# RMSNorm with SiLU: each converting tile transfer cut into eight transfers of every eighth partition

## The chip, the cores and the metric

One core of a Trainium2 chip runs the whole kernel. The metric is device time in microseconds; executions of one kernel agreed within about 1% (1.4% and 1.8% in two of the experiments). The profiled execution of each kernel has its own, slightly shorter span, which the profile's shares refer to. No TensorE work is done, and the granted clock was 1.0.

## The reference

```python
batch, seq_len, hidden = 8, 1024, 2048          # x float32, gamma float32, eps 1e-5
rms = np.sqrt(np.mean(x ** 2, axis=-1, keepdims=True) + eps)
out = gamma * x / rms
return (out * (1 / (1 + np.exp(-out)))).astype(np.float32)
```

8192 rows of 2048 float32: 67.1 MB are read, 67.1 MB written. On the chip the rows are held as bfloat16, and the transfers convert both ways; both kernels issue them from POOL.

## The kernel before

A tile is 128 rows, one per partition. There are 64 tiles, each with one load and one store.

```python
pool = ctx.enter_context(tc.tile_pool(name="pool", bufs=8))
...
for i in range(ntiles):
    ...
    xt = pool.tile([P, d], bf16)
    nc.gpsimd.dma_start(out=xt[:ts], in_=x2[s:e])          # L42: float32 -> bfloat16
    xg = pool.tile([P, d], bf16)
    nc.vector.tensor_mul(out=xg[:ts], in0=xt[:ts], in1=g[:ts])
    ...                                                     # squares on DVE, Sqrt on ACT, reciprocal on DVE
    ot = pool.tile([P, d], bf16)
    nc.scalar.activation(out=ot[:ts], in_=xg[:ts], func=...Silu, scale=rstd[:ts])
    nc.gpsimd.dma_start(out=o2[s:e], in_=ot[:ts])          # L65: bfloat16 -> float32
```

## Time and profile before

| | before |
|---|---|
| time | 338.42 us median of 2 (337.41 to 339.43) |
| span of the profiled execution | 336.1 us |
| transfers issued (all from POOL) | 129 |
| POOL busy | 69.0 us, 21% |
| ACT, DVE busy | 65%, 66% |
| DMA engines' share | 104.1% |

The "share of 16 engines" adds up the time of every packet; since a row's record overlaps the next one's by 20 to 40 ns (records of 324 and 341 ns follow each other every 305 ns), it goes over 100% when the engines are always busy. GB/s counts bytes as they arrive. The prediction shows the lines.

### The profile page before, as it was taken

What the parts mean: (1) busy time and instruction counts of PE and PEld (TensorE: products, weight loads), DVE (VectorE), ACT (ScalarE), POOL (GpSimd) and SP (SyncE); (2) the same over time, 40 slices, a digit from 0 to 9 for tenths busy, and PEclk for the clock granted to TensorE, in tenths of its full rate; (3) what the DMA queues carried; (4) which work ended last, traced back from release to release, by engine and by line L of the source; (5) the groups of instructions that cost most, each with busy time, mean ns of one, the idle gap of its engine ahead of it and who ended that gap; (6) DMA issues with size and microseconds to landing.
All of it is one profiled execution on the core that took longest, in us unless ns stands there. A gap on an engine that the chain in (4) does not pass through costs nothing.

```text
span 336.1 us, 838 instructions
## 1 busy us (share of the span) xinstructions
DVE 221.2 (66%) x257; ACT 219.1 (65%) x188; POOL 69.0 (21%) x133
## 2 busy tenths in 40 slices
DVE  0999990407999914099999030899991308999900
ACT  1486977522869795238697761386978613869792
POOL 6012111050111110501111105011111050111110
DMA  7999999899999998999999989999999799999997
GB/s 140 212 214 254 335 398 363 332 312 208 214 288 327 402 365 321 324 214 214 291 316 414 366 325 310 214 212 319 307 424 367 286 297 214 213 311 309 420 429 273
DMA packets 18582, 101.24 MB, mean 301 GB/s; under 512 B 2064, under 2 KB 2064, under 8 KB 10384
## 3 DMA queue, kind: packets, MB, share of 16 engines
q0 software_dynamic: 18576, 101.20, 104.1%
q14 instruction: 6, 0.05, 0.0%
HBM read 68.16 MB, written 67.11 MB: 402 GB/s over the span
## 4 chain that ended last, share of the span: by engine, by line
issue 72%; POOL 14%; DMA 11%; POOLq 1%; PEldq 0%
DMA xt<-in_x_dram 11%; POOL out_dram L65 10%; POOL xt L42 4%; POOLq L65 0%; POOL g L34 0%; POOLq L96 0%; POOLq L42 0%; PEldq L96 0%
## 5 line engine op out<-in xcount | busy, mean ns | idle before, releaser
L48 DVE CUSTOM_DVE_ANT_0 xt<-xt 128x2048 bf16<-128x2048 bf16 x64 | 144.8, 2280 | 0.3
L45 DVE TENSOR_TENSOR xg<-xt,g 128x2048 bf16<-128x2048 bf16 x64 | 76.6, 1217 | 95.7 <-DMA xt<-in_x_dram 95.7
L62 ACT ACTIVATE ot<-xg,rstd 128x2048 bf16<-128x2048 bf16 x64 | 124.4, 1993 | 5.8 <-DVE rstd L59 5.5
L55 ACT ACTIVATE rms<-ss,eps_t 128x1 f32<-128x1 f32 x64 | 17.8, 292 | 101.8 <-DVE ss L48 63.7
L65 POOL DMA_DIRECT2D out_dram<-ot x64 | 34.2, 534 | 221.4 <-ACT ot L62 221.4
L42 POOL DMA_DIRECT2D xt<-in_x_dram x64 | 34.1, 554 | 38.8 <-DVE ss L48 22.8
L55 ACT ACT_TABLE_LOAD x30 | 38.5, 1283 | 2.1 <-DVE ss L48 1.0
L62 ACT ACT_TABLE_LOAD x30 | 38.5, 1283 | 0.5
L59 DVE RECIPROCAL rstd<-rms 128x1 f32<-128x1 f32 x64 | 8.6, 153 | 8.4 <-ACT rms L55 8.4
L48 DVE DVE_READ_ACCUMULATOR2_ANT ss<- 128x1 f32 x64 | 5.2, 81 | 0.0
L34 POOL DMA_DIRECT2D g<-in_gamma_dram x1 | 0.7, 667 | 0.8 <-PEq L96 0.8
L36 DVE MEMSET eps_t<- 128x1 f32 x1 | 0.1, 59 | 0.8 <-PEq L82 0.8
L82 POOL MEMSET const-float32-0.0<- 128x1 f32 x1 | 0.1, 99 | 0.2 <-issue 0.2
L82 POOL MEMSET const-bfloat16-1.0<- 128x1 bf16 x1 | 0.1, 102 | 0.0
L82 POOL MEMSET const-float32-1.0<- 128x1 f32 x1 | 0.1, 99 | 0.0
L82 POOL MEMSET const-uint8-127<- 128x1 uint8 x1 | 0.1, 99 | 0.0
## 6 DMA issues: line engine op xcount, KB each, us to landing
out_dram<-ot POOLq DMA_DIRECT2D x64, 1024.0 KB, 11.5
xt<-in_x_dram POOLq DMA_DIRECT2D x64, 512.0 KB, 15.5
g<-in_gamma_dram POOLq DMA_DIRECT2D x1, 512.0 KB, 4.7
```

Source lines behind the costliest of these rows:

```text
L34: nc.gpsimd.dma_start(out=g, in_=gbc)
L36: nc.vector.memset(eps_t, float(eps))
L42: nc.gpsimd.dma_start(out=xt[:ts], in_=x2[s:e])
L45: nc.vector.tensor_mul(out=xg[:ts], in0=xt[:ts], in1=g[:ts])
L48: nc.vector.tensor_tensor_reduce(out=xt[:ts], in0=xt[:ts], in1=xt[:ts], scale=1.0, scalar=0.0, op0=mybir.AluOpType.mult, op1=mybir.AluOpTy ...
L55: nc.scalar.activation(out=rms[:ts], in_=ss[:ts], func=mybir.ActivationFunctionType.Sqrt, scale=1.0 / d, bias=eps_t[:ts])
L59: nc.vector.reciprocal(out=rstd[:ts], in_=rms[:ts])
L62: nc.scalar.activation(out=ot[:ts], in_=xg[:ts], func=mybir.ActivationFunctionType.Silu, scale=rstd[:ts])
L65: nc.gpsimd.dma_start(out=o2[s:e], in_=ot[:ts])
L82: nc = _bacc.Bacc("TRN2", target_bir_lowering=False, num_devices=1)
```

## The change

The intent: a load reads 8 KB of float32 per row and writes 4 KB of bfloat16, a store the reverse. If a DMA engine can read for one while it writes for the other, then alternating single load and store rows in every engine would balance its two sides. A tile is therefore moved in eight transfers of 16 rows, which gives each of the 16 engines one row, and stores and loads are issued in turn. With it come 40 buffers, a lead of 28 loaded tiles, work in groups of four tiles, in-place tiles, and half of the squares on ACT.

```diff
+    BUFS, LEAD, GRAIN = 40, 28, 8
+    def rows(t, i, j):
+        return t[i * P:(i + 1) * P].rearrange("(p g) d -> g p d", g=GRAIN)[j]
+    def lanes(t, j):
+        ...
+        return t[j:P:GRAIN]
+    def load(i, j):
+        if j == 0:
+            xts[i] = pool.tile([P, d], bf16, name="xt")
+        nc.gpsimd.dma_start(out=lanes(xts[i], j), in_=rows(x2, i, j))
...
-        xt = pool.tile([P, d], bf16)
-        nc.gpsimd.dma_start(out=xt[:ts], in_=x2[s:e])
+    for i in range(LEAD):
+        for j in range(GRAIN):
+            load(i, j)
...
+        if k % 2 == 0:
+            nc.scalar.activation(out=sq, in_=xts[i], func=ACT.Square, accum_out=acc)
+        else:
+            nc.vector.tensor_tensor_reduce(out=junk, in0=xts[i], in1=xts[i], ...)
...
-        nc.gpsimd.dma_start(out=o2[s:e], in_=ot[:ts])
+            nc.scalar.activation(out=xt, in_=xt, func=ACT.Silu, scale=rstd[:, k:k + 1])
+            for j in range(GRAIN):
+                nc.gpsimd.dma_start(out=rows(o2, i, j), in_=lanes(xt, j))
+                if i + LEAD < ntiles:
+                    load(i + LEAD, j)
```

More of the change, by code (lines that the diff above doesn't have):

```diff
@@ L7 @@
 from concourse._compat import with_exitstack
+ACT = mybir.ActivationFunctionType
+ALU = mybir.AluOpType
 @with_exitstack
@@ L25 @@
     n, d = x2.shape
-    ntiles = (n + P - 1) // P
+    ntiles = n // P
+    BUFS, LEAD, GRAIN = 40, 28, 8
     singles = ctx.enter_context(tc.tile_pool(name="singles", bufs=1))
-    pool = ctx.enter_context(tc.tile_pool(name="pool", bufs=8))
+    pool = ctx.enter_context(tc.tile_pool(name="pool", bufs=BUFS))
     small = ctx.enter_context(tc.tile_pool(name="small", bufs=8))
+    def rows(t, i, j):
+        return t[i * P:(i + 1) * P].rearrange("(p g) d -> g p d", g=GRAIN)[j]
+    def lanes(t, j):
+        if GRAIN == 1:
+            return t
+        return t[j:P:GRAIN]
+    xts = {}
+    def load(i, j):
+        if j == 0:
+            xts[i] = pool.tile([P, d], bf16, name="xt")
+        nc.gpsimd.dma_start(out=lanes(xts[i], j), in_=rows(x2, i, j))
     g = singles.tile([P, d], bf16)
@@ L36 @@
     nc.vector.memset(eps_t, float(eps))
-    for i in range(ntiles):
-        s, e = i * P, min((i + 1) * P, n)
-        ts = e - s
-        xt = pool.tile([P, d], bf16)
-        nc.gpsimd.dma_start(out=xt[:ts], in_=x2[s:e])
-        xg = pool.tile([P, d], bf16)
-        nc.vector.tensor_mul(out=xg[:ts], in0=xt[:ts], in1=g[:ts])
-        ss = small.tile([P, 1], f32)
-        nc.vector.tensor_tensor_reduce(
-            out=xt[:ts], in0=xt[:ts], in1=xt[:ts],
-            scale=1.0, scalar=0.0,
-            op0=mybir.AluOpType.mult, op1=mybir.AluOpType.add,
-            accum_out=ss[:ts],
-        )
-        rms = small.tile([P, 1], f32)
-        nc.scalar.activation(out=rms[:ts], in_=ss[:ts],
-                             func=mybir.ActivationFunctionType.Sqrt,
-                             scale=1.0 / d, bias=eps_t[:ts])
-        rstd = small.tile([P, 1], f32)
-        nc.vector.reciprocal(out=rstd[:ts], in_=rms[:ts])
-        ot = pool.tile([P, d], bf16)
-        nc.scalar.activation(out=ot[:ts], in_=xg[:ts],
-                             func=mybir.ActivationFunctionType.Silu,
-                             scale=rstd[:ts])
-        nc.gpsimd.dma_start(out=o2[s:e], in_=ot[:ts])
+    sq = singles.tile([P, d], bf16)
@@ new lines, with stats @@
+    for i in range(LEAD):
+        for j in range(GRAIN):
+            load(i, j)
+    GROUP = 4
+    var = {}
+    def stats(i):
+        k = i % GROUP
+        if k == 0:
+            var[i // GROUP] = small.tile([P, GROUP], f32, name="ss")
+        acc = var[i // GROUP][:, k:k + 1]
+        if k % 2 == 0:
+            nc.scalar.activation(out=sq, in_=xts[i], func=ACT.Square, accum_out=acc)
+        else:
+            nc.vector.tensor_tensor_reduce(out=junk, in0=xts[i], in1=xts[i], scale=1.0, scalar=0.0,
+                                           op0=ALU.mult, op1=ALU.add, accum_out=acc)
@@ new lines, with norm @@
+    junk = singles.tile([P, d], bf16, name="junk")
+    def norm(b):
+        ss = var.pop(b)
+        rms = small.tile([P, GROUP], f32, name="rms")
+        nc.scalar.activation(out=rms, in_=ss, func=ACT.Sqrt, scale=1.0 / d, bias=eps_t)
+        rstd = small.tile([P, GROUP], f32, name="rstd")
+        nc.vector.reciprocal(out=rstd, in_=rms)
+        for i in range(b * GROUP, (b + 1) * GROUP):
+            nc.vector.tensor_mul(out=xts[i], in0=xts[i], in1=g)
+        for i in range(b * GROUP, (b + 1) * GROUP):
+            k = i % GROUP
+            xt = xts.pop(i)
+            nc.scalar.activation(out=xt, in_=xt, func=ACT.Silu, scale=rstd[:, k:k + 1])
[3 more added lines that the diff above has]
+                    load(i + LEAD, j)
@@ L69 @@
+    for b in range(ntiles // GROUP):
+        for i in range(b * GROUP, (b + 1) * GROUP):
+            stats(i)
+        norm(b)
 _INS = ['x', 'gamma', 'eps']
```

## The prediction

> **What bounds the kernel now.** I read the page's table of slices first, then the DMA queue totals, then the DMA view cut to three stretches, then the groups of instructions and the waits.
>
> The slices and the totals, over the span of 336.1 us:
>
> ```profile
> POOL 6012111050111110501111105011111050111110
> DMA  7999999899999998999999989999999799999997
> GB/s 140 212 214 254 335 398 363 332 312 208 214 288 327 402 365 321 324 214 214 291 316 414 366 325 310 214 212 319 307 424 367 286 297 214 213 311 309 420 429 273
> ...
> q0 software_dynamic: 18576, 101.20, 104.1%
> ```
>
> The DMA row is 9 nearly everywhere, so the sixteen engines are the bound. The GB/s row swings from 212 to 429 while the engines stay equally busy. The view counts bytes as they arrive: a load turns 8 KB of float32 into 4 KB, a store 4 KB into 8 KB. So 212 (all loads) and 429 (all stores) are the same rate of rows: what costs is the float32 side, whichever end it lies on.
>
> The same view in three stretches, all loads (76 to 92 us), mixed (94 to 112 us) and all stores (112 to 122 us):
>
> ```profile
> DMA packets 934, 3.40 MB, mean 212 GB/s; under 512 B 106, under 2 KB 106, under 8 KB 933
> ```
>
> ```profile
> DMA packets 1052, 5.78 MB, mean 321 GB/s; under 512 B 113, under 2 KB 113, under 8 KB 579
> ```
>
> ```profile
> DMA packets 590, 4.28 MB, mean 428 GB/s; under 512 B 66, under 2 KB 66, under 8 KB 68
> ```
>
> Packets under 512 B are the completion packets that end each transfer on each engine; the rest are rows. A row therefore holds an engine for 16 x 16.0 us / 828 = 309 ns in loads, 16 x 10.0 / 524 = 305 ns in stores, and 16 x 18.0 / 939 = 307 ns where both alternate transfer by transfer. All 16512 rows (8192 loads, 8192 stores, 128 of gamma) at 307 ns on 16 engines are 317 us; the other 19 us of the span are the start, the end, and short holes where the engines ran dry (a DMA share of 0.51 between 64 and 68 us, 0.46 between 132 and 136 us).
>
> The instructions that matter, and the waits:
>
> ```profile
> L65 POOL DMA_DIRECT2D out_dram<-ot x64 | 34.2, 534 | 221.4 <-ACT ot L62 221.4
> L42 POOL DMA_DIRECT2D xt<-in_x_dram x64 | 34.1, 554 | 38.8 <-DVE ss L48 22.8
> ```
>
> ```profile
> 1.92 3.72 POOL L42 DMA_DIRECT2D xt<-in_x_dram  x7
> ```
>
> POOL spends 0.53 us to issue one transfer of 128 rows (7 back to back in 3.72 us) and is 21% busy: 129 issues, most of its time idle behind ACT. No engine other than the DMA engines is near its limit (DVE 66%, ACT 65%).
>
> **What the Trainium skill says.** "DMA: Bandwidth & Descriptors", section "Two DMAs through the same engine are not ordered", says that an engine's read and write sides are separate queues and that descriptors are pipelined. That is the hope behind this change: a load reads 8 KB and writes 4, a store reads 4 and writes 8, so a pair needs 12 KB on each side rather than 16, and could take 3/4 of the time. The trace does not agree so far: 307 ns in the mixed stretch against 309 and 305 in the pure ones. The same page, "Anatomy of one DMA — SWDGE (gpsimd) path", says of descriptor generation that "You can emit a lot of descriptors before the incremental cost shows up"; that is, an issue costs nearly the same for few rows as for many. The trace of before has only issues of 128 rows, so it can't confirm it; it decides this case. "Perfetto Trace Analysis", section "What \"DMA-bound\" means", names the issuing engine's solid row of DMA slices as a bound of its own kind. The page on DMA, "The descriptor swizzle", has each engine of a 128-partition transfer on one SBUF port; with every eighth partition, engines n and n+4 would meet on one port. No run here shows that yet.
>
> **The change part by part.**
>
> Removed: 7/8 of the rows of each transfer. Added: 8 times as many transfers. 64 loads and 64 stores become 512 and 512, each of 16 rows, one row to an engine; with gamma 1025 issues. Rows and bytes stay.
>
> 1. Completion packets. Each transfer ends with one on every engine: 129 become 1025 per engine. In the packet records one takes 22 ns behind a load and 42 ns behind a store, and it delays the next row by about 20 ns (loads follow each other every 305 ns; with the completion packet between, 326 ns; a store, the packet, then a load: about 324 to 343 ns). Cost: 896 x 20 ns = 18 us, on the path.
>
> 2. Engine time as a floor. 1024 rows per engine at 326 ns = 334 us, gamma 3 us, first row at 2.7 us, from the last packet to the end about 2 us: 341 us, if the engines never run dry.
>
> 3. Holes removed. The new kernel loads 28 tiles ahead into 40 buffers, so no load waits for DVE or ACT, and a store has its tile ready long before. Loading 28 tiles takes 224 x 0.326 = 73 us; then stores and loads alternate for 36 tiles; then 28 tiles of stores. This takes away most of the 19 us of holes, and is already in step 2 (no hole counted). Steps 1 and 3 about cancel.
>
> 4. ACT and DVE. ACT takes half of the squares: 32 x 2.0 + 64 x 1.99 + 16 x 0.29 + 32 table loads x 1.28 (60 before) = 237 us; DVE 32 x 2.28 + 64 x 1.22 + small = 156 us. Per tile ACT needs 3.7 us, the DMA engines 16 x 0.326 = 5.2 us where both ways run. Both lie beside the transfers: 0.
>
> 5. Eight in flight. In the built program's order each issue waits for the eighth before it (eight semaphores in turn). Before, that was 64 rows per engine in flight, now 8, or 8 x 0.326 = 2.6 us of work. The loop without queueing: landing to POOL's start 0.3 us, issue about 0.4, end of issue to first packet 0.6 (1.10 us from start to first packet at 133.84 us, 0.53 of it the issue), the row 0.33, completion packet to landing 0.3 to 0.4: about 2.0 us. It fits, barely. Cost 0, with a risk.
>
> 6. Issue time. POOL has to issue one transfer per 326 ns or it becomes the bound. With 128 rows it takes 520 to 550 ns. The sixteen engines' first packets after a dry spell start within 0.15 us of one another, some 10 ns apart, which looks like sixteen engines being told in turn: that part does not shrink with the rows. If the rest were all proportional to rows, 16 rows would take 0.15 + 0.38/8 = 0.20 us; if nothing is, 0.52 us. I take 0.40 us as the middle of my belief: the skill's sentence says mostly fixed. Then 1025 x 0.40 = 410 us, plus start and end of about 8 us: 418 us.
>
> Sum: the larger of the engine floor (341) and the issue time (1025 x T + 8, equal at T = 0.325 us).
>
> **The rivals.**
>
> A, overlap is real when single rows alternate: a pair would cost at best 3/4 of 610 ns plus two completion packets, 500 ns. Mixed stretch 36 tiles x 8 x 0.50 = 144 us rather than 188, so 297 us, and only if POOL issues in 0.25 us. For it: two separate sides. Against it: the mixed stretch, and that every turn from load to store in the trace of before, with the same completion packet between, showed a full-length row on both sides. 10%.
>
> B, the engines stay the bound: 335 to 346 us, a draw. Needs T of at most 0.33 us. For it: issues might scale with rows. A shared SBUF port could add a few us. 25%.
>
> C, POOL's issue becomes the bound, T from 0.34 to 0.48 us: 356 to 500 us. 55%. With T at 0.5 us and over, above 500: 10%.
>
> **How the range and chances follow.** Adding up, 10% lie below 331 us, 35% below 346. The middle of the whole lies at T of about 0.36 us, 1025 x 0.36 + 8 = 377; I say 380 us. Eight in ten: from the lower edge of B, 332, to near the upper end of C, 490 us. Faster by over 2% (under 331.7 us): 0.10. Within 2% (to 345.2): 0.25. Slower: 0.65.
>
> **What would show it.** In the page of the changed kernel: completion packets 16 x 1025 = 16400 (sure). POOL's busy share: over 90%, with its issues back to back, under C; around 60 to 90% and waiting for DMA landings under B. The mean ns of the L51 and L93 issues is T itself. The DMA row: 9 throughout under A and B, 6 to 8 under C, from the first slice on, as the loads at the start are issued at the same pace. Under A, the middle of the span, where loads and stores alternate, has more GB/s than the mean of its two ends; under B and C no more than 321. ACT and DVE must stay under 240 and 160 us. The prediction is wrong if the middle stretch moves over 10% more rows per us than the ends with the engines busy, if T is 0.25 us or less, or if the loop of step 5 is longer than 2.6 us, which would show as POOL idle for landings while the DMA row is below 9.

## The result and the profile after

The changed kernel takes 520.49 us (520.27 to 520.70, 2 runs) against 338.42: ratio 1.537, 95% interval 1.531 to 1.542. It is slower by more than half, and outside the predicted range of 332 to 490 us. (A ratio is the mean time of one kernel's fast runs over that of the other's of the same rounds, so it is not quite the ratio of the medians quoted.)

From the page of the changed kernel, the slices, and the totals of the packets:

```profile
POOL 7999989998999989999899989999899998999895
DMA  7989879998788878888788878888788876777675
GB/s 125 133 131 133 134 109 134 134 136 190 183 206 205 198 171 203 206 206 206 171 203 208 203 188 187 206 207 206 169 205 204 260 278 248 273 276 279 244 274 182
...
DMA packets 32927, 101.38 MB, mean 195 GB/s; under 512 B 16400, under 2 KB 16400, under 8 KB 24720
```

POOL, which was at 0 to 2 in most slices, is at 8 or 9 in nearly all. Read the GB/s row in its three parts: only loads at first (131 where before reached 212), both in the middle (206 where before reached 321), only stores at the end (274 where before reached 429). All three fell to 0.62 to 0.64 of what they were: one pace was set for rows of every kind. The chain that ended last, the two issuing lines, and POOL's waits for loads to land, from the waits view (line, what it waited for, us in total, times, longest):

```profile
POOL xt L51 45%; POOL out_dram L93 44%; DMA xt<-in_x_dram 2%; DMA g<-in_gamma_dram 1%; POOLq L131 0%; PEldq L131 0%
...
L51 POOL DMA_DIRECT2D xt<-in_x_dram x512 | 317.3, 659 | 10.8 <-issue 7.1
L93 POOL DMA_DIRECT2D out_dram<-xt x512 | 317.3, 637 | 9.1 <-issue 9.1
...
POOL xt L51 <- DMA xt<-in_x_dram: 1.4, 3, 0.6
```

89% of the chain is POOL issuing, and it hardly ever waited for a landing. One trap here: the mean of 637 to 659 ns is not what an issue costs. Consecutive issues' records overlap, which is why the two groups sum to 634 us in a span of 519. The pace is read from the timeline, where POOL's work is merged:

```profile
6.96 13.47 POOL L51 DMA_DIRECT2D xt<-in_x_dram  x28 [1.65 <-DMA g<-in_gamma_dram]
```

28 issues in 13.47 us are 0.48 us each; over the whole trace the median spacing is 0.475 us. It is the same from 430 us on, when DVE and ACT have nothing left to do, so their work is not what slows POOL. An issue of 16 rows costs nearly what one of 128 rows cost before (7 in 3.72 us, 0.53 each).

Eight times, first after 128 issues and then after every 121, POOL also stopped, so that 1.9 to 3.2 us passed from one issue to the next. One of the stops:

```profile
63.88 2.46 POOL L51 DMA_DIRECT2D xt<-in_x_dram  x5
68.79 3.38 POOL L51 DMA_DIRECT2D xt<-in_x_dram  x7 [2.45 <-issue]
```

The sum: 1024 spacings of 0.475 us are 486 us, the eight stops add 18 us over a normal spacing, about 7 us are the wait for gamma's landing and small gaps, and 7 us lie before the first and after the last issue. That is 518 of 518.9 us.

### The profile page after: what moved, and what is told of

It is laid out like the page before. It is cut to its first block, busy times and chain, and to the rows that moved or that the text cites. A ratio compares the mean times of both kernels' runs of the same rounds, so it can differ in the third digit from the quotient of the medians.

```text
span 518.9 us, 1891 instructions
## 1 busy us (share of the span) xinstructions
DVE 152.3 (29%) x145; ACT 232.3 (45%) x177; POOL 492.5 (95%) x1029
## 2 busy tenths in 40 slices
DMA packets 32927, 101.38 MB, mean 195 GB/s; under 512 B 16400, under 2 KB 16400, under 8 KB 24720
## 4 chain that ended last, share of the span: by engine, by line
POOL 89%; issue 6%; DMA 4%; POOLq 0%; PEldq 0%
POOL xt L51 45%; POOL out_dram L93 44%; DMA xt<-in_x_dram 2%; DMA g<-in_gamma_dram 1%; POOLq L131 0%; PEldq L131 0%
## 5 line engine op out<-in xcount | busy, mean ns | idle before, releaser
L51 POOL DMA_DIRECT2D xt<-in_x_dram x512 | 317.3, 659 | 10.8 <-issue 7.1
L93 POOL DMA_DIRECT2D out_dram<-xt x512 | 317.3, 637 | 9.1 <-issue 9.1
L87 DVE TENSOR_TENSOR xt<-xt,g 128x2048 bf16<-128x2048 bf16 x64 | 77.7, 1224 | 214.0 <-DMA xt<-in_x_dram 137.3
L91 ACT ACTIVATE xt<-xt,rstd 128x2048 bf16<-128x2048 bf16 x64 | 122.8, 1989 | 0.2
L73 ACT ACTIVATE sq<-xt 128x2048 bf16<-128x2048 bf16 x32 | 60.8, 1901 | 65.6 <-DMA xt<-in_x_dram 65.3
L75 DVE CUSTOM_DVE_ANT_0 junk<-xt 128x2048 bf16<-128x2048 bf16 x32 | 73.2, 2287 | 36.3 <-DMA xt<-in_x_dram 36.3
L73 ACT ACTIVATION_READ_ACCUMULATOR sq<-xt 128x1 f32 x32 | 6.0, 186 | 0.0
L85 DVE RECIPROCAL rstd<-rms 128x4 f32<-128x4 f32 x16 | 2.8, 178 | 7.1 <-ACT rms L83 7.1
L83 ACT ACTIVATE rms<-ss,eps_t 128x4 f32<-128x4 f32 x16 | 4.8, 297 | 0.2
L75 DVE DVE_READ_ACCUMULATOR2_ANT ss<- 128x1 f32 x32 | 2.6, 82 | 0.0
```

The source lines that it names most:

```text
L51: nc.gpsimd.dma_start(out=lanes(xts[i], j), in_=rows(x2, i, j))
L73: nc.scalar.activation(out=sq, in_=xts[i], func=ACT.Square, accum_out=acc)
L75: nc.vector.tensor_tensor_reduce(out=junk, in0=xts[i], in1=xts[i], scale=1.0, scalar=0.0, op0=ALU.mult, op1=ALU.add, accum_out=acc)
L83: nc.scalar.activation(out=rms, in_=ss, func=ACT.Sqrt, scale=1.0 / d, bias=eps_t)
L85: nc.vector.reciprocal(out=rstd, in_=rms)
L87: nc.vector.tensor_mul(out=xts[i], in0=xts[i], in1=g)
```

## The experiments

Theory: POOL's nearly fixed time per issue is the bound, so time is the larger of the DMA engines' floor and the number of issues times that cost. Rivals: the other parts of the change cost the time; small transfers cost the engines themselves; every eighth partition is slow to move; and, apart from the time, that alternation does overlap and is only hidden. All runs gave correct results.

### Whole tiles, all else as changed

```diff
-    BUFS, LEAD, GRAIN = 40, 28, 8
+    BUFS, LEAD, GRAIN = 40, 28, 1
```

> The changed kernel with whole tiles of 128 rows in each transfer (129 issues rather than 1025), all else kept: 28 tiles of lead, 40 buffers, squares split between ACT and DVE. Theory (POOL's fixed time per issue, about 0.47 us for 16 rows against 0.52 for 128, is what costs): back to DMA engines as the bound, 320 to 327 us, POOL under 20% busy. Rival (the other parts of the change, the long lead or the regrouped ACT and DVE work, cost the time): stays well above the 338 us of before.

Measured: 324.56 us (before 338.60 in the same rounds; ratio 0.959, 0.957 to 0.960). Its page and its waits:

```profile
POOL 6122112112221221121121122112212212121100
DMA  6999999999999999999999999999999999999996
...
q0 software_dynamic: 18576, 101.20, 107.2%
```

```profile
POOL out_dram L93 <- DMA out_dram<-xt: 98.0, 47, 2.2
POOL xt L51 <- DMA xt<-in_x_dram: 96.6, 56, 2.0
```

(A waits line: engine and line, what it waited for, us in total, times, longest.) POOL is idle again and waits for landings, that is for the DMA engines. The rest of the change is no cost. It is worth 14 us: of the 19 us that the prediction counted for start, end and holes, the holes are gone (the DMA row is 9 throughout). That the long lead did this, rather than the other parts, was not taken apart. With 129 issues as before, undoing the eighths alone takes 196 us away.

### Four and two parts

```diff
-    BUFS, LEAD, GRAIN = 40, 28, 8
+    BUFS, LEAD, GRAIN = 40, 28, 4        # and, in another run, 2
```

> Each tile in four transfers of 32 rows, 513 issues. Theory (a bound: the larger of engine floor and issues times 0.47 us): POOL needs 513 x 0.48 = 246 us and does not bind, so 326 to 338 us, about 331 with 512 completion packets of 21 ns per engine. Rival (every transfer adds its own cost to the path, in proportion to their number): a good 80 us above the kernel with whole tiles, about 405 us.

> Each tile in two transfers of 64 rows, 257 issues, 126 us of POOL. Theory (larger of engine floor and issues): 324 to 330 us, 2 to 4 us above whole tiles by 128 more completion packets per engine and two pauses that eight transfers in flight of 4 rows should cover. Rival (four parts at 342 us lost its time to the transfers' number and not to pauses): 330 us, a third of the way from 324.6 to 342.

Measured: four parts 342.11 us (ratio to before 1.011, 1.009 to 1.013), two parts 326.97 us (0.965, 0.964 to 0.967). Two parts are as the theory has it. Four parts, within 2% of the kernel before, are 11 us over its best estimate and 4 us over its range, far below the 405 us of cost in proportion. POOL made four of its stops in that run, about 3 us each over its usual spacing, and its issues stood 0.515 us apart where they followed at once, so it needs 264 us of 340 (78% busy). Eight transfers of two rows hold at most 5 us of work, of which about 1.7 us is the loop outside the engines; a stop can therefore run them dry, which two parts with four rows each should not let it. That is an estimate, and the trace bears it out. The GB/s row of four parts, from 85 to 238 us, dips after two of the stops, which begin at 82 and 161 us:

```profile
GB/s 185 219 316 313 313 310 309 318 313 316 312 310 309 311 316 317 316 311 310 313 256 186 266 321 314 310 303 311 312 319 311 316 310 313 313 310 315 310 311 313
```

Counted from the packets, some 51 rows start in each us, but as few as 8 to 25 after each of the four stops; what is missing is about 9 us of the engines' work. After the two stops of the run in two parts nothing is missing.

The two runs serve a second end: they alternate loads and stores in runs of four and of two rows with the engines full. The DMA view of the run in two parts, in its load-only (5 to 65 us), mixed (81 to 228 us) and store-only (260 to 315 us) stretch:

```profile
DMA packets 3863, 12.68 MB, mean 211 GB/s; under 512 B 768, under 2 KB 768, under 8 KB 3863
```

```profile
DMA packets 9508, 46.67 MB, mean 318 GB/s; under 512 B 1904, under 2 KB 1904, under 8 KB 5719
```

```profile
DMA packets 3557, 23.33 MB, mean 424 GB/s; under 512 B 710, under 2 KB 710, under 8 KB 710
```

As in the prediction, 16 times the stretch over packets less completion packets: an engine gives a row 310 ns, 309 ns and 309 ns. The same for whole tiles: 308, 307, 306 ns; for four parts: 318, 327, 320 ns (314 to 315 in all three clear of the start and of POOL's stops). Mixing is never the faster one, though with four parts every second row is a turn. The three also give the price of a completion packet. From 20 us on, clear of the start, the load-only stretches of one, two and four parts take 307, 310 and 314 ns per row, with one packet per 8, 4 and 2 rows: 3/8 of a packet more per row costs 8 ns, so about 20 ns each.

### Sixteen parts

```diff
+    BUFS, LEAD, GRAIN = 40, 28, 16
```

> Each tile in sixteen transfers of 8 rows, 2049 issues. Theory (an issue costs POOL about 0.47 us whatever the rows): 2049 x 0.47 = 963 us, and the pauses of 2 to 3 us that POOL made every 121 issues in the changed kernel, 17 x 2.7 = 46 us: about 1010 us. Rival (cost per issue shrinks with its rows, as 0.40 + 0.074 x rows / 16): about 930 us or less; rival (DMA engines or the port they write to are the bound, not issues): about 520 us.

Measured: 1114.6 us (one run). That bears out the theory in its direction, but 100 us more than it said:

```profile
9.57 21.17 POOL L51 DMA_DIRECT2D xt<-in_x_dram  x40
```

An issue of 8 rows is spaced at 0.53 us (0.523 median over the trace), dearer than one of 16. 2049 x 0.523 = 1072 us, plus 15 stops at 1.8 us beyond a normal spacing. Why 8 rows cost more is open; one thing seen is that this run has 49168 packets under 512 B, 1.5 times the 16 x 2049 = 32784 completion packets that one per engine and issue would make. Taken together:

| parts | issues | rows each | spacing of issues that follow at once, us | time, us |
|---|---|---|---|---|
| 1 | 129 | 128 | 0.52 | 324.56 |
| 2 | 257 | 64 | 0.51 to 0.53 | 326.97 |
| 4 | 513 | 32 | 0.515 | 342.11 |
| 8 | 1025 | 16 | 0.475 | 520.49 |
| 16 | 2049 | 8 | 0.523 | 1114.6 |

Rows per issue vary by 16, the cost by a tenth and not in their order. Time is nearly flat while issues times cost stay below the engines' 320 us or so, and follows the issues above.

### Which addresses an eighth takes

Load rows in the changed kernel take 440 ns on the mean in the packet records, those of whole tiles 324 ns; store rows 323 and 339. Three kernels looked for the reason: rows next to one another in DRAM, partitions next to one another in SBUF, or both.

```diff
-        return t[i * P:(i + 1) * P].rearrange("(p g) d -> g p d", g=GRAIN)[j]
+        return t[i * P:(i + 1) * P].rearrange("(g p) d -> g p d", g=GRAIN)[j]   # DRAM
-        return t[j:P:GRAIN]
+        return t[j * (P // GRAIN):(j + 1) * (P // GRAIN)]                       # SBUF
```

> The changed kernel, each eighth being 16 partitions next to one another in SBUF and 16 rows next to one another in DRAM. Load rows in the changed kernel take 440 ns on the mean, against 324 to 332 in others. Theory SBUF port (engines that share a port slow each other; more would share one here): load rows above 600 ns, and the time above 560 us. Theory DRAM pitch (16 rows, 64 KB apart, collide): load rows back near 324 ns, time near 520 us, still bound by issue. Theory dry start (a load row that begins on an engine which had run dry takes longer): load rows as before, about 440 ns, 520 us.

> Every eighth partition in SBUF, but 16 neighbouring rows in DRAM. Time about 520 us under all, bound by issue. Load rows: theory SBUF port, about 440 ns as in the changed kernel; theory DRAM pitch, near 324 ns; theory dry start, about 440 ns.

> Sixteen neighbouring partitions in SBUF, rows 64 KB apart in DRAM. Theory SBUF port: load rows above 600 ns and a time above 560 us; theory DRAM pitch: about 440 ns, 520 us; theory dry start: about 440 ns, 520 us.

Measured (one run each): 520.15, 518.67 and 519.56 us. The time does not care which addresses an eighth takes. Load rows took 419, 430 and 438 ns in the mixed stretch against 458 in the changed kernel, so neither a shared SBUF port nor the pitch in DRAM explains more than a small part. A match of records by their times (the records don't name the engine, so it is rough) fits the third reading: load rows that follow a completion packet directly took 383 ns in the changed kernel, those with nothing before them 513 ns; with four parts 325 and 679 ns, the latter from some 70 rows only. A load that starts on an engine that had run dry seems to pay for its first read. No experiment took this apart. One thing was found on the way: with neighbouring partitions, store rows in the last stretch rose from 325 to 385 ns in both runs that had them, and stayed at 325 with rows neighbouring in DRAM alone.

### Single rows in turn, without the bound at issue

In the mixed tiles, every second tile goes whole, the others in eighths, in turn or in blocks:

```diff
+            if i % 2 == 0 and i + LEAD < ntiles:
+                load_whole(i + LEAD)
+                for j in range(GRAIN):
+                    nc.gpsimd.dma_start(out=rows(o2, i, j), in_=lanes(xt, j))
+                    load(i + 1 + LEAD, j)        # control: in a second loop of its own
+            else:
+                nc.gpsimd.dma_start(out=o2[i * P:(i + 1) * P], in_=xt)
```

> Single rows alternate while issue does not bind: in the 36 tiles where loads and stores both run, one tile in two goes in eighths, store and load eighth in turn, the other in one whole load and one whole store; 381 issues, 180 us of POOL. Theory that an engine does not overlap a store's write with the next load's read: equal to the control with the same transfers in another order within 2 us, both 325 to 333 us. Rival (alternating rows overlap, hidden so far by the issue bound): up to 18 pairs x 8 x 0.15 = 21 us below the control, about 307 us.

> Control of the run with alternating single rows: the same 381 transfers of the same sizes, but eight store eighths, then eight load eighths. Both theories: 325 to 333 us, as many completion packets as there. Its difference to that run is what alternating is worth.

Measured: 384.68 us in turn, 388.84 us in blocks (ratios to before 1.136 and 1.150). Both missed their range by 52 and 56 us, so the test was flawed. Our reading, not tested: an issue waits for the eighth before it, which here is often a whole tile, and POOL could then not refill single rows fast enough. An engine gave a row 416 and 422 ns in the mixed stretch. Alternating was 1% the better of two starved kernels.

A second pair used one cycle of eight issues per tile, with 80 rows and three times 16:

```diff
+    PARTS = [(48, 128), (0, 16), (16, 32), (32, 48)]
+                for j in range(GRAIN):
+                    store(xt, i, j)
+                    load(i + LEAD, j)            # control: in a second loop of its own
```

> Alternating again, with a cycle that fits eight transfers in flight, since the first try ran the engines dry: in the mixed 36 tiles each tile moves as 80 rows and three times 16, store and load in turn; 8 issues per tile, 3.9 us of POOL against 5.1 us of the engines. No overlap in an engine: within 2 us of its control, both 326 to 340 us. Overlap: 3 pairs x 0.15 us x 36 = 16 us below the control.

> Control: the same transfers, but all four parts of a store, then all four of a load. Both theories: 326 to 340 us; its difference to the alternating run is what alternating is worth.

Measured: 361.43 us in turn, 350.64 us in blocks (ratios 1.068, 1.063 to 1.072, and 1.032, 1.024 to 1.041; one of the control's four runs counts as slow and is left out of its ratio). Their mixed stretches (90 to 252 us, and 87 to 243 us):

```profile
DMA packets 10475, 43.12 MB, mean 266 GB/s; under 512 B 3479, under 2 KB 3479, under 8 KB 6946
```

```profile
DMA packets 10827, 44.32 MB, mean 284 GB/s; under 512 B 3602, under 2 KB 3602, under 8 KB 7234
```

371 and 345 ns per row: in turn is the slower, where overlap asked for 16 us less. Both again lie above the range, and why single rows cost this much beside 80-row parts is not settled. So single rows on full engines were not had clean; what the runs show is no gain in runs of 8, 4 and 2 rows with engines full or nearly so, and no clear gain (one small plus, one larger minus) with single rows.

### Half of the issues from another engine

Stores go from SP and do not convert: Silu writes float32 into four tiles of their own, and there are 36 buffers rather than 40.

```diff
+            ot = outs.tile([P, d], f32, name="ot")
-            nc.scalar.activation(out=xt, in_=xt, func=ACT.Silu, ...)
-                nc.gpsimd.dma_start(out=rows(o2, i, j), in_=lanes(xt, j))
+            nc.scalar.activation(out=ot, in_=xt, func=ACT.Silu, ...)
+                nc.sync.dma_start(out=rows(o2, i, j), in_=lanes(ot, j))
```

> The changed kernel with its 512 store eighths issued by SP instead of POOL ([...]Silu writes float32 into four tiles of their own; 36 buffers rather than 40). As many transfers, rows and completion packets; POOL has 513 issues. Theory (POOL's time per issue is the bound): the bound falls to 513 x 0.474 = 243 us and 4 pauses, below the engine floor, so 335 to 365 us. Rival (small transfers themselves, not their issue, hold the engines): stays near 520 us. Single load and store rows also meet in each engine here without a bound at issue, from two queues: overlap of the two would bring it below 320 us.

Measured: 485.97 us (ratio 1.434), 121 us over the theory's range. POOL's share fell from 95% to 51% as it should, the time by 7% only. At the end the new issuer sets the pace:

```profile
379.65 20.80 SPq L95 DMA_DIRECT2D out_dram<-ot  x33
```

That is 0.63 us per store, 207 GB/s, for the last 170 us. Before that, loads went out every 0.61 us rather than 0.475. Nor could SP use the time before:

```profile
SPq L95 <- ACT ot L93: 125.9, 14, 27.8
```

In the built order ACT's squares, which wait for later loads, stand between the Silus, so about half of the tiles were still to be stored when the last load was issued at 314 us. The run therefore does not test the theory cleanly. Two more kernels split it: whole-tile stores from SP with load eighths, and the reverse.

```diff
+            nc.sync.dma_start(out=o2[i * P:(i + 1) * P], in_=ot)          # first: stores whole
+            nc.gpsimd.dma_start(out=xts[i], in_=x2[i * P:(i + 1) * P])    # second: loads whole
```

> Loads in eighths from POOL (513 issues), stores in whole tiles of 1 MB from SP (64 issues). Theory (issue alone is the bound; the other run was held by SP's 0.63 us per store): POOL needs 513 x 0.474 = 243 us and four pauses, the engines 512 x 0.33 + 512 x 0.307 + 8 = 334 us: 332 to 350 us. Rival (single load rows are slow in themselves next to other traffic): loads at the 0.605 us each that the other run shows, 310 us, then what is left of the stores: 370 to 430 us.

> Loads in whole tiles from POOL (65 issues), stores in eighths from SP (512 issues). Theory (SP's issue at 0.632 us is the bound): first store at about 22 us, then 512 x 0.632 = 324 us: 346 to 356 us. Rival (single load rows made the other run slow and SP's issue did not): equal to the engine floor, 330 to 340 us; rival (single rows in either direction are slow next to other traffic): above 380 us.

Measured: 402.52 us and 589.49 us (ratios 1.186 and 1.742). The first lies in the rival's range: POOL has time (62% busy), yet its 512 load eighths take until 378 us, since they wait for one another's landing:

```profile
POOL xt L52 <- DMA xt<-in_x_dram: 110.6, 148, 3.2
```

Eight in flight, landing 4.9 us after issue at the median (3.1 in the changed kernel), are at most one per 0.61 us; the run came to one per 0.74 us on the mean. That need not be a limit of small loads, though. Counted from the packets in steps of 2 us, between 30 and 376 us, the engines started 50 rows per us in the 160 us with a burst of whole-tile stores, about what they reach with whole tiles (16 rows per 307 ns, 52), and 30 in the 88 us without stores, near the 32 of the changed kernel's first part. As we read it, two known limits took turns: engines that the loads share with the stores, and the pace of small loads on their own. Stores come in bursts since four Silus follow one another in this built order. In the run with store eighths as well, the engines started 41 to 46 rows per us in the steps with 10 to 30 store rows per us; why not 52 is open. The second kernel fits none of the three figures and tells nothing of SP's issues: in the built order ACT has the squares of tiles 28 to 40 ahead of the Silu of tile 5, and the loads of tiles 36 and on need a buffer that Silu frees, so stores and loads waited in a circle of dependences:

```profile
SPq L95 <- ACT ot L93: 236.9, 21, 33.3
```

It is an experiment spoiled by the scheduler's order. So what half of the issues on another engine would be worth was not measured. The cause in the changed kernel doesn't hang on it: POOL waited for landings 1.4 us there, in 3 waits.

## Why the prediction was wrong

- **What binds before** held: the engines, at 307 ns per row. So did the reading that the other parts would close the holes: 324.56 us with whole tiles.
- **Step 1, completion packets**: 20 ns foreseen, about 20 measured; their number was 16400 as stated. The engine floor of step 2, 341 us, was never reached, so it could not be tested at eight parts.
- **Step 4 and step 5** held: ACT 232 us and DVE 152 us busy (237 and 156 foreseen), and POOL hardly waited for landings.
- **Step 6 is the step that failed, by size**: "I take 0.40 us as the middle of my belief". It measured 0.475 us, 77 us over 1025 issues. The step assumed that a part of the cost shrinks with the rows; the runs with 8 to 128 rows show 0.47 to 0.53 us with no such trend. The chain's other term, "about 8 us" for start and end, was 7 us, but 18 us of POOL's stops and 7 us of small gaps were not in the sum. 418 + 77 + 25 = 520.
- **The range** then failed for two reasons. Its upper end, 490 us, was set below rival C's, 500 us at T = 0.48: the measured T alone gives 1025 x 0.475 + 8 = 495 us by the prediction's own sum, and the stops and gaps came on top. And the point, 380 us, was the middle of a spread that gave 25% to a cheap issue for which the trace of before had no row; the only issue cost on the page was 0.53. The sum of step 6 itself said 418. The lower edge, 332, is not rival B's either, which was given as 335.
- **Rival A, overlap**, remains unsupported: mixed rows were not clearly faster at any grain.
- **The shared SBUF port**, the prediction's own inference from a page, cost no time: 518.67 to 520.15 us with other addresses.
- **What would show it**: POOL over 90%, back to back, loads slow from the first slice: all seen. That the mean ns of the L51 and L93 issues would be T itself was wrong: their records overlap, 659 and 637 ns against a spacing of 475. The DMA row at "6 to 8" came out mostly at 7 to 9, because load rows grew longer than 324 ns.

## What to carry to other kernels

Before cutting a transfer into pieces, multiply the number of issues by the issue cost that the trace already shows, without a discount for smaller pieces, and compare with the engines' floor; here the cut was nearly free at two parts (2.4 us) and ruinous at eight. Keep the other half of such a change apart: the long lead and whole tiles gave 324.56 us, the best of all kernels run and 4% under the one before. A busy row that is full on an issuing engine and a GB/s row that sinks by one factor in every stretch are the signs.

## What the Trainium skill lacked or had wrong

- "DMA: Bandwidth & Descriptors", "Anatomy of one DMA — SWDGE (gpsimd) path", calls descriptor generation "small, variable". It gives no cost per issue. Here each held POOL for 0.475 us (16 rows) to 0.53 us (128 and 8 rows), nearly fixed, and 1025 of them were the bound. Its remark that many descriptors come before the incremental cost shows up agrees.
- The same section calls the bubble of the semaphore write about one cycle. Here a completion packet, which may be more than that write, delayed an engine's next row by about 20 ns.
- The same page, "Two DMAs through the same engine are not ordered", tells of separate, pipelined read and write sides. No page says whether converting loads and stores gain by alternating; here a row took 309 ns mixed against 310 and 309 ns apart.
- No page that I read has the stop that POOL makes after every 121 issues (1.6 to 4.4 us from one issue to the next), at the same issue numbers with 8, 16, 32 and 64 rows each.
- No page that I read tells what small converting loads cost on engines that also move another stream: here the engines started 41 to 46 rows per us with load eighths beside store eighths, 52 in the run with whole tiles.
